# When the input forms are loaded and when the weight sums are formed, in a two-layer decoder

## The chip, the cores and the metric

The kernel runs on one core of a Trainium2 chip. The metric is the time of one execution on the device in microseconds (us); of several executions the median is given. The engines are TensorE (PE in the profile; PEld is its weight load), VectorE (DVE), ScalarE (ACT), GpSimd (POOL) and SyncE (SP). SP and POOL mostly issue DMA transfers, each through a queue of its own.

## The reference

Two layers, 512 tokens, width 1024, everything in float32. Shapes are left out here where the names tell them.

```python
def hybrid_layer(x, g_mix, w_in, sinks, w_a, w_b, w_out, g_mlp, w_up, w_down):
    h = rmsnorm(x, g_mix)
    aq, ak, av, rq, rk, rv, rg, ga, gb = jnp.split(h @ w_in, SPLIT_POINTS, axis=-1)
    aq, ak = rope_half(aq, pos), rope_half(ak, pos)
    ya = sliding_window_sink_attention(aq, ak, av, sinks) @ w_a     # window 128, 8 heads
    rq, rk = retention_rotation(rq, pos), retention_rotation(rk, pos) * (RET_QK_DIM ** -0.5)
    r = chunkwise_retention(rq, rk, rv)                             # 4 heads, chunks of 128
    r = r * lax.rsqrt(jnp.mean(r * r, axis=-1, keepdims=True) + EPS)
    r = r * jax.nn.silu(rg)
    yb = r @ w_b
    x = x + (jax.nn.sigmoid(ga) * ya + jax.nn.sigmoid(gb) * yb) @ w_out
    h2 = rmsnorm(x, g_mlp)
    return x + jnp.square(jax.nn.relu(h2 @ w_up)) @ w_down

def reference(x, ...):
    for l in range(DEPTH):          # DEPTH = 2
        x = hybrid_layer(x, ...)
    return rmsnorm(x, g_final)
```

## The kernel before

**Products.** Every float32 operand is split into a high and a low part. A product is three matmuls, high by high, low by high and high by low (lines 391 to 393 in `products`), of 128 x 128 weights against 512 or 256 tokens. A weight unit is loaded by SP into one of five `raw` buffers, ScalarE makes its high part (line 339) and DVE its low part (line 340); loads are issued four units ahead. Results stand in five banks of `ps_mm` and three of `ps_aux`.

**Sums of weights.** The value projection of the retention and the two products of the MLP are computed by a form of Strassen's scheme, with fewer products of halves, which needs sums of weight blocks. `sum_steps` forms these sums in DRAM by DMA on POOL's queue: one job is a copy (line 223) of one block, and the accumulation (line 226) of the other block follows with the next job. Jobs are paced by `pace(src)`. Every second call of it makes a *mark*, a copy of one column of `src` on POOL (line 251), and issues a job behind it, so that the queue goes no faster than the computation. While `quiet[0]` is true, `pace` does nothing.

**Input forms.** The scheme also needs sums and differences of quarters of the normalized input. The class `Turned` makes them: `load` brings four blocks of the layer's input from DRAM into `xg` tiles (line 877, issued by POOL; from `xT` in layer 0 and from `spill` in layer 1); `build` scales them on ScalarE (line 887), combines them on DVE (lines 890 to 893) and splits them (lines 411 and 412). This is done in two rounds, `load(0)`, `build(0)`, `load(2)`, `build(2)`. The `xg` tiles come from the pool `big` of six buffers, which the attention (`late`, `whole`, `qlo`) and the gates (`z`) also use. `values` consumes the forms.

**The order in a layer.** First k, v and q of the attention. Then the chunks of gate a (each multiplied into `x` in place), the first pair of retention q and k (`qk(0)`) and the retention gates 0 to 3 (`put_rg`, line 985) are computed as a sequence of chunks, and the attention runs in the background: `advance` lets a step of it in between the matmuls of the chunks. `drain` ends it. Then come the sigmoid of gate a (line 1110) and the silu of gates 0 to 3 (lines 994 and 995, in place), `load(0)`, `qk(1)`, `build(0)`, `load(2)`, gates 4 and 5, the product of the attention with `w_a` (its evictions, line 1136, multiply into `x`, which is called `mixed` there), in it `build(2)`, then `values`, the retention, and the rest of the layer.

**The final order** of each engine's instructions is not the written one: a scheduler with a timeline of its own orders them, and the pools decide which buffer a tile gets. A change of the source therefore also moves instructions that it does not name.

Of the kernel before, what the change touches and what calls it, by code (L numbers as in the profile page):

```python
# [115 lines left out]
def decoder(ctx, tc, xT, x_first, w_in, w_rv, w_a, w_b, w_out, w_up, w_pair, w_down, w_end, tables, decay, band, g_last, out):  # L116
# [125 lines left out]
    quiet = [False]  # L242

    def pace(src):

        if quiet[0]:
            return
        pace_count[0] += 1
        if steps and pace_count[0] % 2 == 0:
            mark = small.tile([P, 1], F32, tag="mark", name="mark", bufs=2)  # L250
            ins = nc.gpsimd.tensor_copy(mark, src[:, 0:1])
            with tc.issue_after(ins.ins):
                if next(steps[0], DONE) is DONE:
                    steps.pop(0)
# [180 lines left out]
    def drain():  # L435
        while background:
            advance()
# [177 lines left out]
    def layer_body(layer):  # L615
# [112 lines left out]
        def attention():  # L728
# [36 lines left out]
            for n in range(NB):  # L765
                w = P if n == 0 else 2 * P
                keys = slice(0, P) if n == 0 else slice((n - 1) * P, (n + 1) * P)
                at = slice(n * P, (n + 1) * P)
                for c in range(4):
                    col = layer * N_Q + 2 * c  # L770
                    ps = bank(ps_aux, "score")
                    for g in range(N_KV):
                        for i, part in enumerate((kh[g], kl[g])):
                            nc.tensor.matmul(  # L774
                                ps[:, g * w : (g + 1) * w], q_s[g][:, c, at], part[:, keys], start=i == 0, stop=i == 1
                            )
                    sm = temp("sm")
                    s3 = sm[:, : 2 * w].rearrange("p (g k) -> p g k", g=2)
                    st = small.tile([P, 8], F32, tag="st", name="st")
                    nm, es, su, rc = (st[:, 2 * i : 2 * i + 2] for i in range(4))  # L780
                    for g in range(N_KV):
                        nc.vector.tensor_tensor_reduce(
                            s3[:, g, :],
                            ps[:, g * w : (g + 1) * w],
                            mask[:, 2 * P - w :],
                            -(HEAD_DIM**-0.5),
                            nsink[:, col + g : col + g + 1],
                            ALU.add,
                            ALU.min,
                            nm[:, g : g + 1],  # L790
                        )
                    nc.vector.tensor_tensor(es, nm, sink[:, col : col + 2], ALU.add)
                    for g in range(N_KV):
                        nc.scalar.activation(
                            s3[:, g, :], s3[:, g, :], AF.Exp, bias=nm[:, g : g + 1], scale=-1.0, accum_out=su[:, g : g + 1]
                        )
                    last_exp[:] = [nc.scalar.activation(es, es, AF.Exp).ins]
                    nc.vector.tensor_tensor(rc, su, es, ALU.add)
                    nc.vector.reciprocal(rc, rc)
                    for g in range(N_KV):  # L800
                        nc.vector.tensor_scalar(s3[:, g, :], s3[:, g, :], rc[:, g : g + 1], None, ALU.mult)
                    pend.append((n, c, sm))
                    if n > 1:
                        pace(sm)
                    if ready and c == 1 + DELAY:
                        weighted(ready.pop())
                    if len(pend) > DEEP:
                        done = pend.pop(0)
                        transposed(*done)
                        if done[1] == 3:  # L810
                            ready.append(done[0])
                    yield
# [47 lines left out]
        def qk(h, rate=1.0):  # L860
            chunk("w_in", layer, xs, put_ret(rk, h), rate)
            chunk("w_in", layer, xs, put_ret(rq, h), rate)
# [3 lines left out]
        class Turned:  # L866


            def __init__(self):
                self.groups = [[slots.four() for _ in range(2)] for _ in range(2)]  # L870
                self.parts = {}

            def load(self, ks):
                self.b = [big("xg") for _ in range(2)]
# [42 lines left out]
        def values(turned):  # L917

            a, c = ([bank(ps_mm, "rv") for _ in range(2)] for _ in range(2))
            b = [bank(pool, "rv") for pool in (ps_mm, ps_aux)]  # L920
            nc.tensor.matmul(b[1], ones, xh[:, 0, :], start=True, stop=True)
            plus, minus = rms_mix.columns, small.tile([P, NB], F32, tag="ncol", name="ncol", bufs=1)
            nc.vector.tensor_scalar(minus, plus, -1.0, None, ALU.mult)

            def multiply(ps, moving, start=True):
                for u in range(2):
                    hi, lo = unit("rv", layer)
                    for m in range(2):
                        at = slice(m * P, (m + 1) * P)
                        pairs = []  # L930
                        for k in range(2):
                            xh_, xl_ = moving[2 * u + k]
                            cols = slice(k * T, (k + 1) * T)
                            pairs.append(((xh_[:, at], xl_[:, at]), (hi[:, cols], lo[:, cols])))
                        products(ps[m], pairs, start and u == 0, u == 1, not start)

            def scale(j, m, sign):
                return (plus if sign > 0 else minus)[:, 2 * j + m : 2 * j + m + 1]

            def keep(j, ps, sign):  # L940
                got = []
                for m in range(2):
                    t = temp("kept")
                    nc.scalar.activation(t, ps[m], AF.Copy, scale=scale(j, m, sign))
                    got.append(t)
                return got

            def put(i, j, ps, sign, kept=None):
                for m in range(2):
                    hi, lo = slots.one(), slots.one()  # L950
                    if kept:
                        nc.vector.scalar_tensor_tensor(kept[m], ps[m], scale(j, m, sign), kept[m], ALU.mult, ALU.add)
                        split(view(hi), view(lo), kept[m])
                    else:
                        split(view(hi), view(lo), ps[m], scale(j, m, sign))
                    rv[i, 2 * j + m] = (hi, lo)

            multiply(a, quarter(0, 0))
            for m in range(2):
                nc.scalar.activation(b[m], a[m], AF.Copy)  # L960
            multiply(c, turned[1])
            five = keep(1, c, -1)
            multiply(b, turned[2], False)
            turned.free(0)
            two = keep(1, b, 1)
            multiply(a, quarter(1, 0), False)
            put(0, 0, a, 1)
            multiply(c, quarter(1, 1), False)
            put(0, 1, c, 1, two)
            multiply(b, turned[3], False)  # L970
            put(1, 1, b, -1, five)
            multiply(b, turned[4], False)
            turned.free(1)
            put(1, 0, b, -1)
# [3 lines left out]
        def put_rg(i):  # L978
            def put(ps):
                if i % 2 == 0:  # L980
                    two = big("z")
                    rg[i], rg_next[i + 1] = two[:, 0, :], two[:, 1, :]
                else:
                    rg[i] = rg_next.pop(i)
                nc.vector.tensor_tensor(rg[i], ps, rstd(), ALU.mult)  # L985
                pace(rg[i])
                if i >= 4:
                    silu(i)

            return put  # L990

        def silu(i):
            s = temp("sig")
            nc.scalar.activation(s, rg[i], AF.Sigmoid)
            nc.vector.tensor_tensor(rg[i], rg[i], s, ALU.mult)
# [9 lines left out]
        class Head:  # L1005
# [24 lines left out]
            def outputs(self, e):  # L1030
# [10 lines left out]
                nc.scalar.activation(r, ps, AF.Copy)  # L1041
                q = temp("sq")
                nc.scalar.activation(q, ps, AF.Square)
                self.rr.append(r)
                self.sq.append(q)
                if e == 1:
# [27 lines left out]
        def retention(pair):  # L1074
# [25 lines left out]
            for head in two:  # L1100
                head.finish()
                yield

        qk(0, PACE)
        for i in range(4):
            chunk("w_in", layer, xs, put_rg(i), PACE)
        drain()
        with tc.issue_after(last_exp[0]):
            for hs in (slice(0, T // 2), slice(T // 2, T)):
                nc.scalar.activation(x[:, :, hs], x[:, :, hs], AF.Sigmoid)  # L1110
            for i in range(4):
                silu(i)
        source = xT if layer == 0 else spill
        turned = Turned()
        turned.load(0)
        quiet[0] = True
        qk(1)
        with tc.issue_after(last_split[0]), tc.issue_after(last_split[1]):
# [23 lines left out]

        load_decay(0)
        values(turned)
        quiet[0] = False
        background.append(retention(0))
        qk(2, 2.0)
        qk(3, 2.0)
# [651 lines left out]
```

## Time and profile before

| | us |
|---|---|
| Time of three runs, median (lowest to highest) | 1482.54 (1482.43 to 1483.81) |
| The profiled execution, its own time | 1483.84 |
| Its span, first to last instruction | 1482.1 |
| PE busy | 1459.7 |
| DVE busy | 1124.0 |
| ACT busy | 943.1 |
| POOL busy | 213.0 |
| Mean granted TensorE clock | 0.995 |

The profile is of one execution. In lists of waits a row gives the waiting instruction, what it waited for, the total, the count and the longest of these waits. In timelines a row gives start and duration; in brackets stands the idle time of the engine just before, and who ended it. In windows a row gives the window, its length, the busy time and number of instructions of PE, PEld, DVE, ACT and POOL, then the granted TensorE clock, the busy share of the DMA engines and the GB/s they moved. In rows of DMA issues the last number is the median time from issue to landing.

### The profile page before, as it was taken

What the parts mean: (1) busy time and instruction counts of PE and PEld (TensorE: products, weight loads), DVE (VectorE), ACT (ScalarE), POOL (GpSimd) and SP (SyncE); (2) the same over time, 40 slices, a digit from 0 to 9 for tenths busy, and PEclk for the clock granted to TensorE, in tenths of its full rate; (3) what the DMA queues carried; (4) which work ended last, traced back from release to release, by engine and by line L of the source; (5) the groups of instructions that cost most, each with busy time, mean ns of one, the idle gap of its engine ahead of it and who ended that gap; (6) DMA issues with size and microseconds to landing.
All of it is one profiled execution on the core that took longest, in us unless ns stands there. A gap on an engine that the chain in (4) does not pass through costs nothing.

```text
span 1482.1 us, 21386 instructions
## 1 busy us (share of the span) xinstructions
PE 1459.7 (98%) x7751; PEld 1259.0 (85%) x7751; DVE 1124.0 (76%) x1697; ACT 943.1 (64%) x1549; POOL 213.0 (14%) x302
## 2 busy tenths in 40 slices
PE   9999999999999999999999998999999999999998
PEld 7887788888889999999888886888888899999997
DVE  6877777966577888888778687877766778888885
ACT  7656556453467777777766575565435777777775
POOL 0111100102101111112201120002031021111120
PEclk9999999999999999999999999999999999999999
DMA  7659643668975676666957595546598277777664
GB/s 260 195 171 272 193 151 123 184 156 251 281 183 191 186 199 181 181 174 184 302 174 218 170 261 166 181 118 178 163 288 237 92 210 196 189 196 188 179 186 146
DMA packets 95867, 287.32 MB, mean 194 GB/s; under 512 B 11152, under 2 KB 11280, under 8 KB 90896
## 3 DMA queue, kind: packets, MB, share of 16 engines
q1 hardware_dynamic: 61392, 171.37, 34.2%
q0 software_dynamic: 33648, 113.26, 33.7%
q8 instruction: 61, 1.00, 0.3%
q10 hardware_dynamic: 720, 1.31, 0.2%
q14 instruction: 46, 0.38, 0.1%
HBM read 246.05 MB, written 107.48 MB: 239 GB/s over the span
## 4 chain that ended last, share of the span: by engine, by line
PE 89%; DMA 5%; ACT 3%; DVE 1%; issue 1%; POOL 0%; POOLq 0%; DVEq 0%; ACTq 0%
PE mm L391 23%; PE mm L393 23%; PE mm L392 23%; PE b L391 3%; PE b L392 3%; PE b L393 3%; PE rv L393 2%; PE rv L392 2%; PE rv L391 2%; PE mm L406 1%; DMA xg<-spill 1%; DMA sums_up<-w_pair_in 1%; PE score L774 1%; DMA sums_down<-w_down_in 1%; DMA xg<-xT_in 1%
## 5 line engine op out<-in xcount | busy, mean ns | idle before, releaser
L339 ACT ACTIVATE hi<-raw 128x1024 fp32r<-128x1024 f32 (+1 forms) x375 | 382.2, 1020 | 290.0 <-PE mm L392 175.5
L340 DVE TENSOR_TENSOR lo<-raw,hi 128x1024 fp32r<-128x1024 f32 (+1 forms) x376 | 438.4, 1173 | 142.9 <-ACT hi L339 142.0
L391 PE MATMUL mm<-xh,hi 128*128 128x512 f32 (+1 forms) x976 | 344.0, 355 | 1.6 <-DVE z L985 1.0
L392 PE MATMUL mm<-xl,hi 128*128 128x512 f32 (+1 forms) x976 | 343.6, 354 | 0.0
L393 PE MATMUL mm<-xh,lo 128*128 128x512 f32 (+1 forms) x976 | 341.6, 355 | 0.0
L391 PE MATMUL mm<-r,hi 128*128 128x256 f32 (+1 forms) x736 | 238.6, 328 | 9.8 <-DVE x L1136 9.4
L393 PE MATMUL mm<-r,lo 128*128 128x256 f32 (+1 forms) x736 | 240.7, 327 | 0.4 <-DVE lo L340 0.4
L392 PE MATMUL mm<-r,hi 128*128 128x256 f32 (+1 forms) x736 | 240.8, 327 | 0.0
L391 PEld LDWEIGHTS mm<-xh,hi 128*128 128x128 f32 x976 | 184.8, 189 | 26.7 <-ACT xh L414 1.4
L392 PEld LDWEIGHTS mm<-xl,hi 128*128 128x128 f32 x976 | 184.8, 189 | 24.4
L393 PEld LDWEIGHTS mm<-xh,lo 128*128 128x128 f32 x976 | 183.8, 189 | 23.8
L391 PEld LDWEIGHTS mm<-r,hi 128*128 128x128 f32 x736 | 141.1, 192 | 24.3 <-DVE x L1136 10.1
L392 PEld LDWEIGHTS mm<-r,hi 128*128 128x128 f32 x736 | 141.1, 192 | 13.5
L393 PEld LDWEIGHTS mm<-r,lo 128*128 128x128 f32 x736 | 140.9, 191 | 12.3 <-DVE lo L340 0.6
L1482 POOL DMA_DIRECT2D y<-eu x56 | 62.7, 1362 | 369.4 <-DVE eu L1467 369.4
L392 PE MATMUL mm<-lo,r 128*128 128x512 f32 (+1 forms) x276 | 104.3, 387 | 0.0
L393 PE MATMUL mm<-hi,r 128*128 128x512 f32 (+1 forms) x276 | 101.2, 387 | 0.0
L391 PE MATMUL mm<-hi,r 128*128 128x512 f32 (+1 forms) x276 | 98.7, 391 | 0.5 <-ACT r L411 0.2
L391 PE MATMUL b<-hi,r 128*128 128x512 f32 x180 | 70.5, 392 | 0.0
L392 PE MATMUL b<-lo,r 128*128 128x512 f32 x180 | 70.3, 391 | 0.0
L393 PE MATMUL b<-hi,r 128*128 128x512 f32 x180 | 67.8, 389 | 0.0
L275 DVE TENSOR_TENSOR raw<-raw 128x512 f32<-128x512 f32 x56 | 38.5, 688 | 37.4 <-DMA raw<-w_pair_in 26.3
(298 smaller groups left out, 2405.6 us busy)
## 6 DMA issues: line engine op xcount, KB each, us to landing
raw<-w_in_in SPq DMA_DIRECT2D x73, 512.0 KB, 4.3
sums_down<-w_down_in POOLq DMA_DIRECT2D x30, 1024.0 KB, 11.3
sums_up<-w_pair_in POOLq DMA_DIRECT2D x56, 512.0 KB, 11.0
raw<-w_down_in SPq DMA_DIRECT2D x45, 512.0 KB, 7.6
raw<-w_pair_in SPq DMA_DIRECT2D x84, 256.0 KB, 3.7
y<-y POOLq DMA_DIRECT2D x62, 256.0 KB, 9.3
y<-eu POOLq DMA_DIRECT2D x62, 256.0 KB, 8.2
raw<-sums_down SPq DMA_DIRECT2D x30, 512.0 KB, 7.4
```

The source lines that it names most:

```text
L275: nc.vector.tensor_tensor(raws[i][:, at], last[:, LEFT], last[:, RIGHT], ALU.add)
L339: state["high"] = nc.scalar.activation(hi[:, at], raw[:, at], AF.Copy).ins
L340: nc.vector.tensor_tensor(lo[:, at], raw[:, at], f32(hi[:, at]), ALU.subtract)
L391: nc.tensor.matmul(ps, ah, bh, start=start and i == 0, stop=False, **more)
L392: nc.tensor.matmul(ps, ah, bl, start=False, stop=False, **more)
L393: latest[0] = nc.tensor.matmul(ps, al, bh, start=False, stop=stop and i == n - 1, **more).ins
L406: latest[0] = nc.tensor.matmul(ps, w[:, cols(j, c)], moving[k][low], start=first, stop=bool(final)).ins
L774: nc.tensor.matmul(ps[:, g * w : (g + 1) * w], q_s[g][:, c, at], part[:, keys], start=i == 0, stop=i == 1)
L1482: nc.gpsimd.dma_start(y[:, 2 * j + m, i * T : (i + 1) * T], t, **how)
```

## The change

It moves the first load of the input forms, and it changes which computations pace the sum jobs.

- `load(0)` is issued behind the second retention gate (`i == 1`), and not behind the attention's end. For this the making of a `Turned` is parted: `take` allocates the slots for its results later, where they were allocated before.
- In the attention `pace(sm)` is called for every odd `c` of all four blocks, and not for all `c` of the last two: eight calls either way.
- The gates 0 to 3 no longer call `pace`; `values` calls it for each result, and the retention's heads for each output `r`.
- `quiet` ends after the first two results of `values`, and not behind all of them.

The number of jobs, of marks and of matmuls stays. The diff, cut to its core:

```diff
                     pend.append((n, c, sm))
-                    if n > 1:
+                    if c % 2:
                         pace(sm)
...
             def __init__(self):
+                self.parts = {}
+
+            def take(self):
                 self.groups = [[slots.four() for _ in range(2)] for _ in range(2)]
-                self.parts = {}
...
                     rv[i, 2 * j + m] = (hi, lo)
+                    pace(f32(view(hi)))
...
             put(0, 1, c, 1, two)
+            quiet[0] = False
             multiply(b, turned[3], False)
...
                 nc.vector.tensor_tensor(rg[i], ps, rstd(), ALU.mult)
-                pace(rg[i])
                 if i >= 4:
+                    pace(rg[i])
                     silu(i)
...
                 nc.scalar.activation(q, ps, AF.Square)
+                pace(r)
...
+        source = xT if layer == 0 else spill
+        turned = Turned()
         qk(0, PACE)
         for i in range(4):
             chunk("w_in", layer, xs, put_rg(i), PACE)
+            if i == 1:
+                turned.load(0)
         drain()
...
-        source = xT if layer == 0 else spill
-        turned = Turned()
-        turned.load(0)
+        turned.take()
         quiet[0] = True
...
         values(turned)
-        quiet[0] = False
         background.append(retention(0))
```

Lines behind the second hunk move down: 877 becomes 879, 985 becomes 989, 995 becomes 999, 1136 becomes 1143.

**POOL, layer 0, around the first loads of the input forms.** `mark`s are the pacing copies, `late` is a tile with a retention q or k, `z` a gate. Before:

```order
L251 COPY mark_1279<-late_89 128x1
L223 DMA sums_down0_93<-w_down_in 128x2048
L226 DMA sums_up0_91<-w_pair_in 128x1024
L251 COPY mark_1369<-z_1321 128x1
L223 DMA sums_up0_91<-w_pair_in 128x1024
L226 DMA sums_down0_93<-w_down_in 128x2048
L877 DMA xg_1473<-xT_in 128x1024
L877 DMA xg_1474<-xT_in 128x1024
L251 COPY mark_1455<-z_1421 128x1
L223 DMA sums_up0_91<-w_pair_in 128x1024
L226 DMA sums_up0_91<-w_pair_in 128x1024
L877 DMA xg_1572<-xT_in 128x1024
```

and now, with the first marks in `values` (`r0`) at the end:

```order
L251 COPY mark_1170<-late_89 128x1
L223 DMA sums_up0_91<-w_pair_in 128x1024
L226 DMA sums_up0_91<-w_pair_in 128x1024
L879 DMA xg_1369<-xT_in 128x1024
L879 DMA xg_1370<-xT_in 128x1024
L251 COPY mark_1279<-late_89 128x1
L223 DMA sums_down0_93<-w_down_in 128x2048
L226 DMA sums_up0_91<-w_pair_in 128x1024
L879 DMA xg_1564<-xT_in 128x1024
L879 DMA xg_1565<-xT_in 128x1024
L251 COPY mark_2039<-r0_81 128x1
L223 DMA sums_up0_91<-w_pair_in 128x1024
```

The first two loads stand ahead of the mark on the second `late` and no longer behind two marks on gates, and no job stands between the second two loads and the values.

**PE, layer 0, the attention's last product.** `pv` is the product of the attention's weights with v, `mm_1523` (before) and `mm_1515` (now) are the second chunk of `qk(1)`, `mm_1475` (now) the first. Before:

```order
L759 MATMUL pv_1381<-r6_87,r3_84 128x512
L391 MATMUL mm_1523<-xh_76,hi_1375 128x512
L759 MATMUL pv_1388<-r6_87,r3_84 128x512
L392 MATMUL mm_1523<-xl_77,hi_1375 128x512
L760 MATMUL pv_1381<-r7_88,r3_84 128x512
L759 MATMUL pv_1381<-r6_87,r3_84 128x512
L760 MATMUL pv_1381<-r7_88,r3_84 128x512
L760 MATMUL pv_1388<-r7_88,r3_84 128x512
```

and now:

```order
L759 MATMUL pv_1381<-r6_87,r3_84 128x512
L392 MATMUL mm_1475<-xl_77,hi_1325 128x512
L759 MATMUL pv_1388<-r6_87,r3_84 128x512
L393 MATMUL mm_1475<-xh_76,lo_1326 128x512
L760 MATMUL pv_1381<-r7_88,r3_84 128x512
L759 MATMUL pv_1381<-r6_87,r3_84 128x512
L760 MATMUL pv_1381<-r7_88,r3_84 128x512
L760 MATMUL pv_1388<-r7_88,r3_84 128x512
```

The last product of the attention stands one chunk of `qk(1)` earlier, 23 chunk matmuls.

**DVE, layer 0, the first build of the input forms.** `xg` and `t2` are its tiles, `rot` are the rotated retention q and k, `lo` the low parts of weights, `x_75` the gate that `w_a`'s result is multiplied into. Before:

```order
L890 TENSOR_TENSOR xg_1474<-xg_1474,xg_1473 128x2x256
L340 TENSOR_TENSOR lo_1615<-raw_1477,hi_1614 128x1024
L412 TENSOR_TENSOR r2_83<-rot_1508,r2_83 128x512
L891 SCALAR_TENSOR_TENSOR t2_1561<-xg_1473,xg_1474 128x512
L412 TENSOR_TENSOR r2_83<-rot_1548,r2_83 128x512
L892 TENSOR_TENSOR xg_1473<-xg_1473 128x2x256
L893 SCALAR_TENSOR_TENSOR xg_1474<-t2_1561,xg_1474 128x2x256
L340 TENSOR_TENSOR lo_1650<-raw_1517,hi_1649 128x1024
L412 TENSOR_TENSOR r0_81<-t2_1561,r0_81 128x512
L412 TENSOR_TENSOR r0_81<-xg_1473,r0_81 128x512
L1136 TENSOR_TENSOR x_75<-x_75,mm_1653 128x512
L412 TENSOR_TENSOR r6_87<-xg_1474,r6_87 128x1024
```

and now:

```order
L892 TENSOR_TENSOR xg_1370<-xg_1370,xg_1369 128x2x256
L340 TENSOR_TENSOR lo_1571<-raw_1423,hi_1570 128x1024
L636 TENSOR_TENSOR rot_1540<-mm_1515,tab_1158 128x512
L637 TENSOR_TENSOR rot2_1541<-rot2_1541,tab_1158 128x512
L893 SCALAR_TENSOR_TENSOR t2_1553<-xg_1369,xg_1370 128x512
L412 TENSOR_TENSOR r2_83<-rot_1500,r2_83 128x512
L638 TENSOR_TENSOR rot_1540<-rot_1540,rot2_1541 128x512
L894 TENSOR_TENSOR xg_1369<-xg_1369 128x2x256
L895 SCALAR_TENSOR_TENSOR xg_1370<-t2_1553,xg_1370 128x2x256
L412 TENSOR_TENSOR r0_81<-t2_1553,r0_81 128x512
L340 TENSOR_TENSOR lo_1607<-raw_1469,hi_1606 128x1024
L412 TENSOR_TENSOR r2_83<-rot_1540,r2_83 128x512
```

The build begins earlier in DVE's order: the second rotation and the split of `raw_1423`, which stood ahead of it, now stand inside it, and the split of `raw_1517`, which stood inside, behind it.

## The prediction

> **What bounds the kernel now.** I read the page first, then the waits of PE, the chain, the timeline at the two long waits, and the windows around them.
>
> ```profile
> span 1482.1 us, 21386 instructions
> PE 1459.7 (98%) x7751; PEld 1259.0 (85%) x7751; DVE 1124.0 (76%) x1697; ACT 943.1 (64%) x1549; POOL 213.0 (14%) x302
> PE 89%; DMA 5%; ACT 3%; DVE 1%; issue 1%; POOL 0%; POOLq 0%; DVEq 0%; ACTq 0%
> ```
>
> TensorE (PE) is busy for 98% of the span and carries 89% of the chain. The change takes no matmul away, so only PE's idle time and its slow stretches can be won: 1482.1 − 1459.7 = 22.4 us idle. The waits of PE say where that is (total, times, longest):
>
> ```profile
> PE mm L391 <- DVE x L1136: 9.4, 2, 5.9
> PE pv L759 <- DVE r L412: 1.6, 1, 1.6
> PE mm L391 <- DVE z L985: 1.0, 1, 1.0
> ```
>
> Two waits, one in each layer, make up 9.4 us. Both stand in the product with `w_a`, at the first matmul that needs a bank which DVE's line 1136 empties. The chain tells why DVE was late (start, length):
>
> ```profile
> 138.11 12.04 DMA sums_down<-w_down_in
> 151.27 11.60 DMA xg<-xT_in
> 162.90 1.34 ACT xg L887 x2
> ...
> 318.22 0.91 PE mm L391 x4
> ...
> 888.53 13.57 DMA xg<-spill
> 902.13 1.34 ACT xg L887 x2
> ```
>
> In layer 0 a weight-sum transfer ends, only then GpSimd (POOL) issues the load of `xg`, which lands 11.60 us later, and ScalarE scales it (line 887). Layer 1 is alike. The timeline shows both ends of it (start, length, idle before and who ended it):
>
> ```profile
> 162.90 2.13 ACT L887 ACTIVATE xg<-xg,x 128x512 f32<-128x512 f32 x3 [7.92 <-DMA xg<-xT_in]
> 902.13 1.34 ACT L887 ACTIVATE xg<-xg,x 128x512 f32<-128x512 f32 x2 [10.16 <-DMA xg<-spill]
> 173.85 0.79 PE L391 MATMUL mm<-r,hi 128*128 128x512 f32 x1 [3.51 <-DVE x L1136]
> 909.27 0.80 PE L391 MATMUL mm<-r,hi 128*128 128x512 f32 x1 [5.86 <-DVE x L1136]
> 165.67 0.69 DVE L890 TENSOR_TENSOR xg<-xg 128x512 f32<-128x512 f32 x1 [7.69 <-ACT xg L887]
> ```
>
> DVE meets the line-890 work ahead of the `w_a` evictions in its queue, so the evictions stood behind it. Without the wait for the load, ScalarE would have started at 162.90 − 7.92 = 154.98 and 902.13 − 10.16 = 891.97. The waits also cost PE speed (window, length, PE busy and its count, ..., granted clock):
>
> ```profile
> 170.23:172.73 2.50, 0.11 (x1) 0.00 (x0) 2.50 (x5) 2.38 (x3) 0.00 (x0) 1.00 0.23 95
> 172.73:173.85 1.12, 0.00 (x1) 0.01 (x1) 1.12 (x3) 1.12 (x3) 0.27 (x1) 0.50 0.85 187
> 173.85:179.56 5.71, 5.71 (x14) 4.46 (x14) 5.21 (x7) 2.18 (x4) 0.26 (x1) 0.50 0.47 147
> 909.27:913.59 4.32, 4.32 (x11) 3.41 (x11) 4.32 (x7) 3.68 (x5) 0.54 (x1) 0.52 0.22 84
> ```
>
> In the chain four matmuls take 0.91 us, 0.2275 each. After the first wait the clock is 0.50 and 13 whole ones (the 14th is cut by the edge) take 5.71 us: 5.71 − 13 × 0.2275 = 2.75 us lost. After the second, 4.32 − 10 × 0.2275 = 2.05 us.
>
> **The loads of `xg`.** The change issues them behind the second retention gate, on the same POOL queue but two jobs earlier. There they stand behind the mark on `late`, one job and its accumulation. `late` is written here:
>
> ```profile
> 123.93 0.62 ACT L411 ACTIVATE late<-rot 128x512 fp32r<-128x512 f32 x1
> 862.23 0.63 ACT L411 ACTIVATE late<-rot 128x512 fp32r<-128x512 f32 x1 [0.33 <-DVE rot L638]
> 109.93 0.68 DVE L412 TENSOR_TENSOR r<-whole,r 128x512 fp32r<-128x512 f32 x1
> 888.53 1.54 POOL L877 DMA_DIRECT2D xg<-spill  x2
> xg<-xT_in POOLq DMA_DIRECT2D x4, 512.0 KB, 12.0
> xg<-spill POOLq DMA_DIRECT2D x4, 512.0 KB, 13.9
> ```
>
> The buffers come from the `big` pool; the last of their old users ends at 109.93 + 0.68, before the mark. So the issue moves from 151.27 to about 123.93 + 0.62 + 1.5 = 126 (1.5 is my estimate for the mark and two issues, from the 1.54 of the last POOL row), and the landing to 126 + 12.0 = 138. ScalarE wants it at 154.98: 17 us to spare. In layer 1: 862.23 + 0.63 + 1.6 = 864.5, landing 878.4, wanted at 891.97. If the accumulation ahead has to sit out a full sum transfer of 12.04 first, the landings are 150 and 890.4, still in time. So the waits on the load go.
>
> What is late next is the DVE chain itself. It would reach the first `w_a` eviction 7.69 us earlier in layer 0, where PE waited 3.51. In layer 1 ScalarE's 10.16 stands against 5.86. In the new order the second rotation of `qk(1)`, three operations of some 0.69 us each like the line-890 row, stands inside the build and not ahead of it; that takes 2.1 of the room, and for such shifts I leave 0.2 us of wait. Won: **9.4 + 2.75 + 2.05 = 14.2 us**. Ends: 14.2, and 14.2 − 1.6 − 2.05 = 10.5, if a longer shift of this kind leaves 1.6 us in layer 1 and the clock falls there anyway.
>
> A rule speaks against counting the 2.75. The Trainium skill ("TensorE: Matmul & The Clock Gate", section on the HAM clock gate) says that half rate follows at least one idle window of about 3.4 us, of a free-running clock: a wait of 3.51 us would then hardly ever hold a whole window, the drop in layer 0 would have had some other cause, and the sum would be 2.75 smaller. The trace differs: the rows have 0.50 from 172.73, 2.4 us into the wait, and no other drop near it. I follow the rows.
>
> **The marks.** `put_rg` no longer makes marks for gates 0 to 3. A mark is a one-column copy on POOL which reads the gate, and the in-place silu on DVE has to wait until it is done:
>
> ```profile
> 144.92 0.69 DVE L995 TENSOR_TENSOR z<-z,sig 128x512 f32<-128x512 f32 x1 [4.71 <-POOL mark L251]
> 890.30 0.69 DVE L995 TENSOR_TENSOR z<-z,sig 128x512 f32<-128x512 f32 x1 [2.07 <-POOL mark L251]
> 146.36 0.47 PE L759 MATMUL pv<-r,r 128*128 128x512 f32 x1 [1.57 <-DVE r L412]
> 868.57 0.50 PE L391 MATMUL mm<-xh,hi 128*128 128x512 f32 x1 [0.97 <-DVE z L985]
> ```
>
> DVE sat 4.71 us behind the mark, its next split was late, and PE waited 1.57 for that. In layer 1 the 0.97 stands in the same stretch. Both go: **1.6 + 1.0 = 2.6 us**; the two DVE waits themselves are off the path. The number of jobs is unchanged, so POOL itself gets neither more nor less.
>
> **The attention comes earlier.** With other marks in the queue the scheduler puts the last attention product 23 chunk matmuls earlier on PE in layer 0: 23 × 0.2275 = 5.2 us. The matmuls are the same, but the first stretch is denser:
>
> ```profile
> 52.75:91.24 38.49, 38.49 (x194) 32.36 (x192) 29.00 (x96) 21.10 (x59) 3.49 (x5) 1.00 0.62 190
> ```
>
> DVE is busy 29.00 of 38.49 us there, 75%. The same work in 38.49 − 5.2 = 33.3 us is 87%, still below full, but single waits may appear. The nearest row is the 1.57 above. I charge one such wait, 1.6, between ends of 0 and two in each layer (6.3); that it gains is not excluded, since an earlier end of the attention gives the DVE chain more room, but that room has no wait left to fill.
>
> **The sum jobs later.** Jobs that were started around the gates start beside the second half of the values and the retention. By the orders some 5 more of them fall between 210 and 310 us:
>
> ```profile
> 210.00:310.00 100.00, 100.00 (x483) 84.84 (x482) 74.39 (x105) 58.14 (x89) 9.48 (x15) 1.00 0.58 166
> 345.00:430.00 85.00, 85.00 (x379) 70.26 (x378) 49.99 (x65) 35.57 (x47) 14.22 (x24) 1.00 0.97 272
> sums_down<-w_down_in POOLq DMA_DIRECT2D x30, 1024.0 KB, 11.3
> sums_up<-w_pair_in POOLq DMA_DIRECT2D x56, 512.0 KB, 11.0
> ```
>
> A job moves its size twice, as copy and as accumulation: 2 × 1024 or 2 × 512 KB, with two of the small ones to each large one 1.4 MB in the mean. Five make 7 MB, or 70 GB/s over these 100 us: 166 + 70 = 236 GB/s. From 345 to 430 us the engines move 272 GB/s at a share of 0.97 and PE is busy for 85.00 of 85.00 us. So I cost it at nothing: the cover is the weights' lead of four units. Its price without that cover is the third rival's.
>
> One job now also starts near 783 us in layer 1, beside the 64 KB shifts of the tile `qlo`, whose landings the trace gives as
>
> ```profile
> DMA to landing us min/median/max: 1.9/2.8/7.0
> ```
>
> If one takes 7.0 for 2.8, a score waits up to 4.2 us. I take 0, by the median, and keep 4.2 as the end.
>
> **The sum.** 14.2 + 2.6 − 1.6 − 0.2 = 15.0 us. The profiled execution took 1483.84 us (1.7 outside its span), so 1483.84 − 15.0 = 1468.8. It lies 1.3 above the median of the runs, 1482.54: **1467.5 us**. About 0.2%, 3 us, is what a measurement of this kernel can tell from no change.
>
> **The rivals.**
>
> *One long wait stays.* The loads land in time, but in one layer the DVE chain (the rotation inside it, a late buffer, a load of 13.9 behind a full transfer) still makes PE wait. For it: in layer 1 the worst landing, 890.4, is only 1.6 ahead of 891.97. Against it: that needs the accumulation to wait a whole transfer. The price is up to 5.86 + 2.05 = 7.9: 1467.5 + 7.9 = 1475.4.
>
> *The loads come no earlier.* If their buffers are held until the attention ends, the order on POOL means nothing. Only the 2.6 of the marks remain: 1482.5 − 2.6 = 1479.9. Against it stands the row at 109.93: the buffers' last reader ends long before.
>
> *Slower: the moved jobs starve the weights.* A unit of the value product holds 12 matmuls of 0.2275 = 2.7 us, and loads are issued four units ahead, 10.9 us. The row to fear is
>
> ```profile
> raw<-w_out_in SPq DMA_DIRECT2D x16, 512.0 KB, 13.1
> raw<-w_rv_in SPq DMA_DIRECT2D x12, 512.0 KB, 4.1
> ```
>
> where loads fall beside dense jobs. Were the value loads (4.1 now) to take 13.1, each of the last 4 units would come 2.2 us late, 8.8, with a half-clock stretch of some 2.4 behind: 11.2 a layer, 22.4 in all. Then 1467.5 + 22.4 = 1489.9. It decides against the change from a landing of 10.9 + 15.0 / 8 = 12.8 us, and only then. Against it: the jobs begin only with the last two of the six products, and the 236 GB/s. The Trainium skill ("DMA: Bandwidth & Descriptors", section on queues, rings and completion order) says that each DMA engine goes round its queues packet by packet, by which a second busy queue halves a load's rate; the median of 4.1 for `w_rv` would then become about 8, still below 10.9, which is no loss. No row here shows the two together at this place.
>
> **How the numbers follow.** The forecast as summed has 0.62, the one long wait 0.18, the loads no earlier 0.08, the slower case 0.12. The forecast's own range is 1464 (no wait from the denser attention, −1.8, and some other idle time won) to 1472 (the 1.6 with a clock drop, or two waits more). To leave out no more than 2 in 10 the range takes in the long wait: 1464 to 1478. The loads no earlier lie at the edge of the 0.2%, half and half: faster 0.62 + 0.18 + 0.04 = 0.84, same 0.04, slower 0.12.
>
> **What would show it.** Right: the waits of PE without line 1143 (the old 1136); the `xg` loads issued near 126 and 864 and no ScalarE wait on them; granted clock 1.00 from 165 to 180 and 900 to 915; no DVE wait on a mark near 145 and 890; `w_rv` landings below 10.9. Wrong: a PE wait of over 2 us in the first attention blocks, or on `lo` (line 340) between 185 and 310 us, which would mean that the weights came late.

## The result and the profile after

The change takes 1466.54 us (median of four runs, 1465.44 to 1468.53), before 1483.17 beside it; the ratio is 0.9888, with a 95% interval of 0.9871 to 0.9905. Predicted were 1467.5 us, from 1464 to 1478, and 0.84 for faster. The profiled execution took 1466.77 us.

The page of the changed kernel begins:

```profile
span 1465.0 us, 21388 instructions
...
PE 1453.4 (99%) x7751; PEld 1256.2 (86%) x7751; DVE 1124.7 (77%) x1697; ACT 944.6 (64%) x1549; POOL 209.0 (14%) x302
...
PE 97%; DMA 1%; ACT 1%; DVE 0%; issue 0%; SPq 0%; DVEq 0%; ACTq 0%
```

The span is 17.1 us shorter. PE's busy time fell by 1459.7 − 1453.4 = 6.3 and its idle time by 22.4 − 11.6 = 10.8. The chain, which went through PE for 89%, now does so for 97%. All waits of PE that the profile still lists, 4.5 of the 11.6 us of idle time (total, times, longest):

```profile
PE turn L1554 <- DMA y<-eu: 1.2, 1, 1.2
PE warm L371 <- DVE ones L366: 1.1, 1, 1.1
PE mm L391 <- ACT xh L414: 1.0, 1, 1.0
PE mm L393 <- DVE lo L340: 0.5, 1, 0.5
PE mm L391 <- ACT mm L1343: 0.5, 1, 0.5
PE mm L391 <- ACT r L411: 0.2, 1, 0.2
```

The two waits at `w_a`, the one at `pv` and the one on `z` are gone. POOL's and ScalarE's timelines show the loads and the first build (line 877 is now 879, line 887 now 889):

```profile
119.45 0.18 POOL L251 COPY mark<-late 128x1 f32<-128x1 f32 x1 [10.85 <-ACT st L797]
...
120.59 0.82 POOL L226 DMA_DIRECT2D sums_up<-w_pair_in  x1 [0.16 <-issue]
121.14 1.38 POOL L879 DMA_DIRECT2D xg<-xT_in  x2
...
133.15 0.90 POOL L226 DMA_DIRECT2D sums_up<-w_pair_in  x1
148.11 0.56 POOL L879 DMA_DIRECT2D xg<-xT_in  x1 [14.06 <-DVE r L412]
...
852.38 1.38 POOL L879 DMA_DIRECT2D xg<-spill  x2
```

```profile
146.36 2.55 ACT L889 ACTIVATE xg<-xg,x 128x512 f32<-128x512 f32 x4
...
877.52 2.55 ACT L889 ACTIVATE xg<-xg,x 128x512 f32<-128x512 f32 x4
...
894.84 1.34 ACT L889 ACTIVATE xg<-xg,x 128x512 f32<-128x512 f32 x2 [2.54 <-DMA xg<-spill]
```

The loads are issued at 121 and 852 us where they were issued at 151 and 889, and ScalarE begins the first build of both layers with no idle time ahead of it (no bracket). In the second build of layer 1 it still waits 2.54 us for a load, which PE does not feel. Between 134 and 148 us POOL issues no sum job. The windows of the changed kernel (the window, its length, PE, PEld, DVE, ACT, POOL, clock, DMA share, GB/s):

```profile
52.75:86.00 33.25, 33.25 (x174) 28.18 (x173) 27.04 (x94) 20.14 (x58) 6.12 (x13) 1.00 0.86 252
165.00:180.00 15.00, 15.00 (x68) 12.43 (x67) 12.18 (x16) 6.89 (x10) 0.00 (x0) 1.00 0.10 36
890.00:910.00 20.00, 20.00 (x90) 16.63 (x90) 18.22 (x25) 9.93 (x13) 0.53 (x1) 1.00 0.23 77
210.00:310.00 100.00, 100.00 (x483) 84.84 (x482) 76.81 (x109) 57.38 (x89) 17.95 (x33) 1.00 0.84 226
```

PE is busy for the whole of each and the clock is 1.00. The moved jobs lifted the stretch from 210 to 310 us from 166 to 226 GB/s, and PE lost nothing there.

### The profile page after: what moved, and what is told of

Its sections match the earlier page's. It is cut to its first block, busy times and chain, and to the rows that moved or that the text cites. A ratio compares the mean times of both kernels' runs of the same rounds, so it can differ in the third digit from the quotient of the medians.

```text
span 1465.0 us, 21388 instructions
## 1 busy us (share of the span) xinstructions
PE 1453.4 (99%) x7751; PEld 1256.2 (86%) x7751; DVE 1124.7 (77%) x1697; ACT 944.6 (64%) x1549; POOL 209.0 (14%) x302
## 4 chain that ended last, share of the span: by engine, by line
PE 97%; DMA 1%; ACT 1%; DVE 0%; issue 0%; SPq 0%; DVEq 0%; ACTq 0%
PE mm L391 25%; PE mm L393 25%; PE mm L392 25%; PE b L391 3%; PE b L392 3%; PE b L393 3%; PE rv L391 2%; PE rv L392 2%; PE rv L393 2%; PE mm L406 1%; PE score L774 1%; PE pT L739 1%; PE r L393 1%; PE r L392 1%; PE r L391 1%; DMA y<-eu 1%
## 5 line engine op out<-in xcount | busy, mean ns | idle before, releaser
L1488 POOL DMA_DIRECT2D y<-y x56 | 55.6, 1007 | 78.7 <-ACT y L1483 73.5
```

The lines of the kernel that those rows point to most:

```text
L1488: nc.gpsimd.dma_start(y[:, 2 * j + m, i * T : (i + 1) * T], t, **how)
```

## The experiments

The theory at first was the prediction's: the place of the load on POOL's queue brings most of it (A). The rival was that the jobs which no longer start on the gates bring it, wherever the load stands (B). The time of the kernel before lay between 1483.2 and 1485.3 us in the several comparisons, so the ratios are what compares.

| kernel | us | ratio to before | 95% interval |
|---|---|---|---|
| the change | 1466.54 | 0.9888 | 0.9871 to 0.9905 |
| loads_only | 1472.15 | 0.9918 | 0.9905 to 0.9932 |
| pace_only | 1467.21 | 0.9883 | 0.9870 to 0.9897 |
| old_attn_marks | 1469.26 | 0.9894 | 0.9880 to 0.9907 |
| pace_old_attn | 1470.44 | 0.9902 | 0.9883 to 0.9920 |
| late_loads | 1468.49 | 0.9891 | 0.9877 to 0.9904 |
| late_old_attn | 1468.46 | 0.9886 | 0.9872 to 0.9901 |
| late_one_job | 1468.57 | 0.9903 | 0.9885 to 0.9920 |
| late_jobs | 1484.40 | 0.9990 | 0.9980 to 0.9999 |
| marks_no_jobs | 1467.33 | 0.9889 | 0.9873 to 0.9905 |
| crowded | 1475.50 | 0.9933 | 0.9914 to 0.9953 |

**loads_only: the early load without the new pacing.**

```diff
 # the kernel before
+            if i == 1:
+                turned.load(0)
...
-        turned.load(0)
+        turned.take()
```

> Of the change only the early first load (its second, sixth and seventh part without the pacing); all marks as before. In the order of POOL the loads then stand ahead of the mark on the second late tile. Theory A (the load's place on the queue brings the 14.2): no PE wait at the w_a evictions, no half clock, but the marks on gates 0 to 3 and their PE waits (1.6 and 1.0) stay: 1466.5 + 2.6 = about 1469. Theory B (the marks taken off the gates bring it, the load's place is of no account): the xg loads still land late, about 1480.

Measured: 0.9918, 1472.15 us. The waits of PE, and of ScalarE for the loads:

```profile
PE rv L391 <- DVE x L1140: 1.4, 1, 1.4
...
PE mm L391 <- DVE z L987: 1.0, 1, 1.0
```

```profile
ACT xg L889 <- DMA xg<-xT_in: 7.9, 1, 7.9
ACT xg L889 <- DMA xg<-spill: 7.4, 1, 7.4
```

The early load alone wins 0.82%, most of the change, and no wait over 1.4 us is left at PE. B's 1480 falls as a statement that the load's place is of no account. But ScalarE still waits over 7 us twice, for the second loads of each layer.

**pace_only: the new pacing without the early load.**

```diff
 # the change
-            if i == 1:
-                turned.load(0)
...
         turned.take()
+        turned.load(0)
```

> The change with the first load put back behind the attention's end; the new pacing stays. POOL's order then has the loads behind the mark on the second late tile and one job, but no gate marks ahead. Theory A (the load must be issued at the second gate): the xg waits return, only the marks' 2.6 is won, about 1480. Theory B (the queue is free early enough without the gates' jobs): issue at about 134 and 865, landing at 138 to 146 and 870 to 879, ScalarE wants them at 146 and 875, so at most a wait of 4 us on ScalarE that PE does not feel: 1466 to 1469.

Measured: 1467.21, 0.9883, which can't be told from the change's 0.9888. PE's longest wait in it is the 1.1 us at the start, and ScalarE's waits for the loads are 1.9 and 0.3. So A falls as well, as a statement that the load must be issued early: with the new pacing, its place in the code is worth nothing that these runs can tell. Either half removes the long waits at `w_a`; with the pacing alone no wait at `w_a`, at `pv` or on `z` is left.

**late_loads: the load really held back, with the new pacing.** In pace_only the load was issued at 134 us, ahead of the attention's end. Here a copy from the attention's result into the buffer stands ahead of it.

```diff
 # pace_only
                     k = ks + 4 * part
+                    if ks == 0:
+                        nc.gpsimd.tensor_copy(b[:, 0, 0:1], f32(a_h[:, 3, T - 1 : T]))
                     nc.gpsimd.dma_start(b, source[:, k : k + 2, :])
```

> The change with the first load behind the attention's end and really held there: a one-column copy from the attention's result into each xg buffer stands ahead of the load on POOL. Issue at about 149 and 880. If the lateness of this load by itself is what cost the two PE waits: landing 4 to 12 us later, ScalarE waits 6 to 14 us from 146 and 875, PE waits that less the room of about 4 at w_a in each layer, 2 to 10, and where that is over 2.4 the half clock adds 2 to 3: 1471 to 1490, most likely 1478. If PE does not wait at w_a with a late load, the explanation by the load falls: 1467.

Measured: 1468.49, 0.9891. The most likely time of the expectation, 1478, was some 10 us too high. The timelines of POOL and ScalarE, and the landings of the `xg` loads in the first layer:

```profile
148.49 0.77 POOL L880 COPY xg<-r 128x1 f32<-128x1 f32 x2 [12.52 <-ACT r L411]
149.20 1.62 POOL L881 DMA_DIRECT2D xg<-xT_in  x3
```

```profile
154.08 2.63 ACT L891 ACTIVATE xg<-xg,x 128x512 f32<-128x512 f32 x4 [1.41 <-issue]
```

```profile
DMA to landing us min/median/max: 3.8/5.2/6.2
```

The load is issued at 149.20, only 2.07 us earlier than in the kernel before (151.27), and nothing that these runs can tell is lost, since it lands after 5.2 us in the median and not after 12.0. So it is not the lateness of the issue alone that cost. ScalarE waits 1.41 us ahead of the first build, and 3.52 us for a load in layer 1; PE has no wait at `w_a`.

**late_jobs: the same, with the sum jobs of the gates put back.**

```diff
 # late_loads
-                if i >= 4:
-                    pace(rg[i])
-                    silu(i)
+                pace(rg[i])
+                if i >= 4:
+                    silu(i)
```

> The held load of late_loads again, and the marks of gates 0 to 3 put back, so that two sum jobs are issued in the 15 us ahead of the load and are in flight beside it. If it is these jobs that make a late load cost: the load is issued near 151 and 882 and lands after 10 to 14 us and not after 4 to 6, ScalarE waits 8 to 12, PE waits 3 to 7 at w_a in each layer with a half clock behind, and the marks' waits of up to 2.6 come back: 1478 to 1487. If the load's lateness counts alone and the jobs do not: as late_loads, 1468.5, plus at most 2.6.

Measured: 1484.40, 0.9990: the whole gain is gone. The timeline of POOL, the waits of PE, and the landings in the first layer (the profiled execution, 1487.50 us, was the slowest of ten):

```profile
142.12 0.53 POOL L223 DMA_DIRECT2D sums_up<-w_pair_in  x1 [0.26 <-issue]
149.10 0.84 POOL L226 DMA_DIRECT2D sums_up<-w_pair_in  x1 [6.46 <-DMA sums_up<-w_pair_in]
...
150.79 1.64 POOL L881 DMA_DIRECT2D xg<-xT_in  x3 [0.31 <-POOL xg L880]
```

```profile
PE mm L391 <- DVE x L1144: 7.2, 1, 7.2
PE mm L391 <- DVE z L991: 6.3, 1, 6.3
```

```profile
DMA to landing us min/median/max: 3.8/13.6/14.6
```

The issue moved by 1.6 us against late_loads (150.79 for 149.20), the landing by 13.6 − 5.2 = 8.4. Both waits of PE are at the first matmul of a bank in the product with `w_a`, one in each layer, and the clock behind them was 0.53 (175.18 to 180.50 us) and 0.50 (912.12 to 917). In layer 0 the bank was emptied by the eviction of a gate, line 991, which stood behind the build in DVE's queue. The waits at `pv` and on a mark, which were expected to come back, did not. The accumulation of a sum, issued at 149.10, is in flight beside the loads. In the kernel before it was alike, 0.5 us ahead of the load at 151.27:

```profile
150.74 0.80 POOL L226 DMA_DIRECT2D sums_down<-w_down_in  x1 [5.39 <-DMA sums_down<-w_down_in]
```

A rival would be that the load only stands behind the accumulation in POOL's own queue. But SP's loads of weight sums in the same 17 us, from 148 to 165, are slow too, first in late_jobs, then in late_loads:

```profile
raw<-sums_rv SPq DMA_DIRECT2D x1, 512.0 KB, 9.2
```

```profile
raw<-sums_rv SPq DMA_DIRECT2D x2, 512.0 KB, 4.8
```

So at least a part of the delay is shared by the queues; how much POOL's own order adds is not shown. This is the mechanism: **two sum jobs on the gates put transfers on the DMA engines exactly when the input forms are fetched, and the fetch is late enough to feel it.** With the same jobs and an early fetch (loads_only) or a late fetch without them (late_loads) no wait of over 1.4 us is left at PE.

**late_one_job: one job in place of two.**

```diff
 # late_loads
-                if i >= 4:
+                if i < 2 or i >= 4:
                     pace(rg[i])
+                if i >= 4:
                     silu(i)
```

> Between late_loads (no job on gates 0 to 3, 1468.5) and late_jobs (two, 1484.4): one job, on gate 1, and the load held to the attention's end. If the crowding by the jobs in flight sets the landing, one job that is nearly through by 149 us costs part: landing 6 to 10, a PE wait of 0 to 3 at w_a: 1469 to 1475. If any mark on a gate costs it all: 1482 or more.

Measured: 1468.57, 0.9903. The accumulation and the load on POOL's timeline, PE's wait, and the landings in the first layer:

```profile
138.53 0.83 POOL L226 DMA_DIRECT2D sums_down<-w_down_in  x1 [4.04 <-DMA sums_down<-w_down_in]
...
147.04 1.11 POOL L881 DMA_DIRECT2D xg<-xT_in  x2
```

```profile
PE mm L391 <- DVE x L1145: 1.2, 1, 1.2
```

```profile
DMA to landing us min/median/max: 3.9/7.5/9.4
```

A job whose accumulation was issued 8.5 us ahead of the load costs a wait of 1.2. It is the second job, still in flight, that costs the rest.

**marks_no_jobs: the marks without the jobs.**

```diff
 # the change
+                if i in (1, 3):
+                    mark = small.tile([P, 1], F32, tag="mark", name="mark", bufs=2)
+                    nc.gpsimd.tensor_copy(mark, rg[i][:, 0:1])
```

> The change with the two one-column copies of gates 1 and 3 put back on POOL, but no sum job behind them. If a mark by itself delays the silu (the prediction's 2.6 us), the DVE waits on a mark and the PE waits of 1.6 and 1.0 come back: 1469. If the copies only waited because the accumulation of a job stood ahead of them on POOL, DVE waits less than 1 us on them and the time is that of the change: 1466 to 1467.5.

Measured: 1467.33, 0.9889. No DVE wait on such a copy and none of the PE waits came back, so a mark on a gate by itself costs nothing that these runs can tell. The copies are short, and no accumulation that waits for its transfer stands ahead of them:

```profile
135.66 1.05 POOL L992 COPY mark<-z 128x1 f32<-128x1 f32 x1
141.69 0.18 POOL L992 COPY mark<-z 128x1 f32<-128x1 f32 x1 [4.99 <-DVE z L989]
```

In the kernel before one stood directly ahead of the mark for which DVE waited 4.71 us:

```profile
143.89 0.81 POOL L226 DMA_DIRECT2D sums_up<-w_pair_in  x1 [5.23 <-DMA sums_up<-w_pair_in]
```

**old_attn_marks, pace_old_attn and late_old_attn: the attention's part.** Each is the change, pace_only or late_loads with the attention's marks as before:

```diff
-                    if c % 2:
+                    if n > 1:
                         pace(sm)
```

> The change without its first part: the attention's marks stay on all c of blocks 2 and 3. The attention's last product stands again where it stood before on PE. If the denser attention costs the 1.6 us that the prediction charged, this is 1.6 faster than the change, about 1465; if it costs nothing, the same within 1 us; if the earlier end of the attention is needed for the build, a PE wait of 0.2 to 1.6 at w_a comes back, 1467 to 1470.

> Of the change only the marks moved from the gates to the values and the retention's outputs; the load in its old place, the attention's marks as before. If these moved marks alone carry the change: 1467 to 1470, no PE wait at w_a. If the load's place or the attention's marks are needed as well: one wait of 3 to 6 at w_a comes back, 1472 to 1480.

> The held load with an empty queue as in late_loads, and the attention's marks as before, so that the attention ends 23 matmuls later on PE. If the empty queue is enough: landing again 4 to 6.5 us, PE waits at w_a of 0 to 2 only, 1468 to 1471. If the earlier end of the attention is what saved late_loads: PE waits 3 to 6 in each layer with the half clock, 1476 to 1482.

Measured: 0.9894, 0.9902 and 0.9886, against 0.9888, 0.9883 and 0.9891 with the new marks; the intervals of each pair overlap. The attention's marks can't be told from no change, and old_attn_marks was not faster by the 1.6 us. pace_old_attn has one wait at `w_a`, of 0.6, late_old_attn none. In late_old_attn the load is issued later than in the kernel before (151.27), and still lands after 6.1 us in the median:

```profile
154.21 1.64 POOL L881 DMA_DIRECT2D xg<-xT_in  x3
```

So the earlier end of the attention is not what saved late_loads. The lists of PE's waits of the three kernels have one thing in common, in the first of them:

```profile
PE mm L391 <- DVE z L989: 1.0, 1, 1.0
```

with 1.1 in the second and 1.0 in the third. This is the wait of 1.0 that the prediction put down to the gates' marks. None of the three has marks on gates 0 to 3; all have the attention in its old order. The wait is also there in loads_only and crowded, which lack the new marks in the attention too (line 987), and in none of the kernels with the new marks. So it goes with the attention's order.

**crowded: the slower rival.** No marks in the attention, and one job for every call from the second half of `values` to the end of `qk(3)`.

```diff
 # the change
-        if steps and pace_count[0] % 2 == 0:
+        if steps and (dense[0] or pace_count[0] % 2 == 0):
...
-                    if c % 2:
-                        pace(sm)
...
+        dense[0] = True
         values(turned)
...
         qk(3, 2.0)
         drain()
+        dense[0] = False
```

> The change without the attention's marks, and with a job at every call (not every second) from the second half of values to the end of the third and fourth retention q and k: twice as many jobs there as in the change. It tests the slower rival. If the weights' lead of four units covers, w_rv landings stay below 10.9 and PE waits on low parts stay below 1 us in all: 1465 to 1469. If the rival holds: w_rv and w_in landings of 13 and more there, PE waits on lo (line 340) of 2.2 us a unit, 10 to 25 us in all: 1477 to 1492.

Measured: 1475.50, 0.9933, between the two. In turn the waits of PE, the wait of DVE, the landings of `w_in` in the windows from 215 to 250 and from 250 to 320 us, where the jobs are dense, and POOL's timeline:

```profile
PE r L392 <- DVE r L412: 3.5, 1, 3.5
...
PE mm L393 <- DVE lo L340: 0.2, 1, 0.2
```

```profile
DVE z L997 <- POOL mark L251: 8.0, 1, 8.0
```

```profile
raw<-w_in_in SPq DMA_DIRECT2D x4, 512.0 KB, 12.7
```

```profile
raw<-w_in_in SPq DMA_DIRECT2D x4, 512.0 KB, 10.5
```

```profile
1020.98 0.81 POOL L226 DMA_DIRECT2D sums_up<-w_pair_in  x1 [14.26 <-DMA sums_up<-w_pair_in]
1021.51 0.47 POOL L251 COPY mark<-z 128x1 f32<-128x1 f32 x1
```

The weights did come more slowly, 12.7 and 10.5 us against 4.3 in the kernel before as a whole, but PE waited only 0.2 on low parts and was busy for 70.00 of the 70 us of the second window: the lead covered them. `w_rv`, which the rival named, is no test, since in layer 0 all its loads are issued by 199 us, ahead of the dense stretch. What costs is POOL's queue: a copy takes over 14 us, the accumulation that waits for it blocks POOL, a mark stands behind that, and a silu in place waits 8.0 us for the mark. The price is PE's 3.5 us and a clock of 0.68 in the window behind it:

```profile
1018.00:1022.00 4.00, 1.48 (x10) 1.24 (x8) 0.00 (x0) 0.00 (x0) 1.02 (x3) 1.00 1.04 248
1022.00:1026.00 4.00, 3.04 (x9) 2.46 (x10) 2.31 (x5) 2.40 (x5) 0.44 (x1) 0.68 1.01 228
```

## Why the prediction was right, and where its steps were not

- **The waits at `w_a`, 9.4, and the half clock, 2.75 + 2.05.** Gone, as said. PE's busy time fell by 6.3, of which these 4.8 are the larger part; where the other 1.5 went no row shows. By the rule of the Trainium skill ("TensorE: Matmul & The Clock Gate", section on the HAM clock gate) the 2.75 would have stayed. The clock of 1.00 from 165 to 180 us agrees with the row that was followed.
- **Why they are gone.** This step was right only in part. Issuing the loads two jobs earlier is enough to remove the long waits (loads_only), but not needed (pace_only, late_loads). What costs is a late load together with the jobs in flight beside it (late_jobs, and the kernel before); taking away either is enough. The row `xg<-xT_in ... 12.0` was read as the load's own duration; it was its duration beside the jobs, and 5.2 without. The prediction counted the landing as fixed and the issue as the lever. That the earlier issue was enough was argued rightly. That a second lever, which the change moves as well and the prediction did not count, left the sum as it was, is luck.
- **The issue times.** 126 and 864.5 were worked out, 121.14 and 852.38 came. `late` was written at 118.70 in place of 123.93, since the attention moved forward; in layer 1 some 8 us of the difference are the time won in layer 0 (its first score starts at 780.3 and no longer at 788.2).
- **The marks' 2.6.** Both waits went, but the reasons were wrong. The 1.0 goes with the attention's order. The mark itself costs nothing that can be told (marks_no_jobs). The 4.71 us of DVE behind it in the kernel before were the accumulation ahead of it in POOL's order, which itself waited 5.23 us for its transfer. What took PE's 1.6 away is not shown: in loads_only the jobs and marks are as before, a silu still waits up to 2.9 us for a mark, and the 1.6 is gone as well.
- **The denser attention, −1.6, and the 0.2 left at the build.** Neither came. DVE was busy 27.04 of 33.25 us, 81% and not 87%, and PE did not wait. The difference from the old attention lies inside the noise. These are the mis-sized terms: without them the sum gives 1467.5 − 1.8 = 1465.7, and measured were 1466.54, so the error is small either way.
- **The moved jobs at nothing.** Right: 226 GB/s (236 were expected), PE 100.00 of 100.00. The nothing for the shifts of `qlo` held too: PE has no wait on a score.
- **The rivals.** One long wait that stays: did not occur. Loads that come no earlier: they came 30 and 36 us earlier. Its price was wrong all the same: held back to the attention's end, with no jobs beside them, they cost nothing that can be told (late_loads), and not 12 us. The starved weights: with twice the jobs the loads slowed to 12.7 us, but PE did not wait for them; there the blocked POOL queue was the bound.

What stays open: why loads_only is 4.4 us slower than the change by the ratios (0.0030 of 1483). Between the two profiled executions it is 5.1 us. Its two PE waits make up 2.4 of these. Another 2.2 are there before any edit matters: the attention's first score, a matmul, starts at 55.0 us and not at 52.8, since its first matmuls took nearly twice as long. In the change:

```profile
5.57 1.17 PE L391 MATMUL mm<-xh,hi 128*128 128x512 f32 x4 [0.97 <-ACT xh L414]
```

And in loads_only:

```profile
5.49 2.04 PE L391 MATMUL mm<-xh,hi 128*128 128x512 f32 x4 [0.64 <-ACT xh L414]
```

The profiled executions of late_loads, late_old_attn, late_jobs and marks_no_jobs start late in the same way (first score at 54.5 to 54.8), so this looks like a property of the execution and not of the edit. One profile for each kernel cannot show whether the other runs of loads_only have it.

## What to carry to other kernels

A load's time to land in a profile is that of its surroundings: before moving a late load, look at what else is in flight beside it, and try to take that away. An edit that does two things at once may owe everything to either, or need only one of them; undo each by itself, and hold the load back on purpose, before the credit is given. Pace background transfers on work that lies in stretches with slack, not on the steps just ahead of a fetch that others wait for.

## What the runs showed of the hardware

A 512 KB load of `xg` landed after 5.2 us in the median with no sum issued in the 14 us ahead of it (late_loads), after 7.5 with an accumulation issued 8.5 us ahead (late_one_job), and after 13.6 with one issued 1.7 us ahead (late_jobs). Loads on SP's queue slowed as well: 9.2 against 4.8 us beside that accumulation, 10.5 to 12.7 us for `w_in` beside the dense jobs of crowded. A copy of one column on POOL took 0.18 to 1.05 us in the rows above, but a DVE instruction that had to follow it waited 8.0 where the copy stood behind an accumulation that waited for its transfer. In crowded PE stood for 3.5 us and the clock was 0.68 in the window behind it; in the kernel before it was 0.50 after 3.51.
